# A trunk kernel's inverses by transposes of 128 rows, and its output projection with two operand halves side by side

## The chip, the cores and the metric

The kernel runs on one core of a Trainium2 chip. The metric is the device time of one execution in microseconds. The kernel before has a median of 2547.64 us over 3 runs (2542.07 to 2549.25). One more execution was profiled; all durations below are from it.

## The reference

A two-layer backbone over 256 latent tokens and 256 context tokens, width 2048, in float32. The even layer joins neighbourhood attention (8 heads) and multi-head latent attention (8 heads), gated by SiLU. The odd layer is a bidirectional chunked gated DeltaNet with 32 value heads and chunks of 64 tokens; only the latent tokens leave it. At the end stands an RMSNorm. For the change two pieces matter:

```python
lmat = jnp.where(strict, jnp.einsum('bhncd,bhnsd->bhncs', kb, kf) * decay, 0.0)
rhs = jnp.concatenate([vf * bf[..., None], kb * jnp.exp(gf)[..., None]], axis=-1)
sol = lax.linalg.triangular_solve(lmat + jnp.eye(CHUNK, dtype=F32), rhs, left_side=True, lower=True)
...
o = rmsnorm(o.transpose(0, 2, 1, 3), o_norm)
return (o.reshape(b, t_len, DN_MIX_WIDTH) * jax.nn.silu(z)) @ w_out
```

The first solves a unit lower triangular system of 64x64 for each head, chunk and direction; the kernel computes the inverse matrices instead. The second is the output projection from 4096 to 2048 channels over the 256 latent tokens.

## The kernel before

Activations lie with channels on the 128 partitions and tokens along the columns. A float32 product is made of three matmuls in a reduced format: both operands are split into a high part and a remainder, and `dense` adds high x high (L90), high weight x remainder (L91) and remainder weight x high (L92) into one PSUM tile. Weights come by DMA in pieces of 128x1024 (`raw`, four buffers); ScalarE (ACT) makes the high part (`whi`, L77 or L1091), VectorE (DVE) the remainder (`wlo`, L78 or L1099). The high and remainder parts of the activations are two tiles of 128 x 16 x 512 numbers, `hh` and `hl`; `ch` and `qr`, and `gh` and `gl`, later take the same two places (tags "hh" and "hl"). A place is free for its next tile when the last reader of the tile before is done.

The run has these stages, with their time in the profiled execution:

- Up to about 700 us: layer-one projections and the neighbourhood attention. At its end `ch` (the latent projections in two parts, L451 and L452) and `qr` (rope queries; its unused rows are filled with zeros by L464) take the places of `hh` and `hl`.
- 700 to 880 us: latent attention, eight heads. The last heads read `qr` in the scores (L348). Then `gh` (L485) and `gl` (L486) are made from the gated results `goA` and `goB`.
- 880 to 1110 us: the first output projection, by 512 columns, and the norm of layer two.
- 1110 to 1760 us: the DeltaNet heads. For each of 16 key heads: projections of k and q with convolution (L566) and activation, then the strictly triangular products of a chunk, `NT` (L744), and the intra-chunk products `sp` (L746). Two heads together give 32 matrices of 64x64 for one `inverse`, eight inverses in all. A scheduler in the framework sets the order on each engine, from the code's order and its own model of durations; within one engine the order is fixed in the built program, and an instruction that waits holds everything behind it on that engine.
- 1760 to 2420 us: the scan over chunks, with its order written out by hand for PE, DVE and ACT; its last steps (58 to 69) also hold the first part of the output projection, `early`: eight units by 24 k-steps.
- 2420 to 2549 us: the rest of the output projection (eight units by 8 k-steps, eight by 32, alternating), the final norm and the stores.

An `inverse` works on all 128 partitions: a diagonal block of 32x32 of the two in a 64x64 matrix stands on the upper 64 partitions in columns 0 to 31 (block 0), on the lower 64 in columns 32 to 63 (block 1). Two transposes of 64 rows (L764) bring the blocks into `L`, so that 31 elimination steps (L778 and L780) run along the free dimension on all matrices at once. POOL multiplies the result `X` by the betas (L782; in the last inverse DVE does). Four more transposes of 64 rows, two by L785 and two by L787, put X and its transpose into `U`, each block back in its own columns. PE makes the off-diagonal block from products (L798 and L815), ACT copies it into `U` (L819), and `by_chunk` (L591) stores `U` to `spu` in DRAM, in eight DMAs of 32 rows by 4 KB. The scan loads `spu` in pieces of 64 columns (256 bytes): `ra`, `rb`, `re`.

In the output projection the operand is `hh` and `hl` seen as 32 k-blocks of 256 tokens; `dense` there issues three matmuls of 256 columns per k-step. `project` (L617) adds a unit's PSUM tile, times the gate, to the residual, in two DVE operations of 128x128.

```python
for b in range(2):
    r = slice(64 * b, 64 * b + 64)
    V.transpose(L[r], NTu[r, :, 32 * b:32 * b + 32].rearrange("p u i -> p i u"))
...
def by_chunk(dst, src):
    for b in range(2):
        for h in range(2):
            nc.sync.dma_start(dst[64 * h + 32 * b:64 * h + 32 * b + 32], src[quad(b, h)])
```

Of the kernel before, what the change touches and what calls it, by code (L numbers as in the profile page):

```python
# [26 lines left out]
def trunk_kernel(ctx: ExitStack, tc: tile.TileContext, g):  # L27
# [57 lines left out]
    def dense(ps, w, off, kt, xh, xl, k0=0, sl=slice(0, T), first=True, last=True):  # L85
        for k in range(kt):
            c = off + k * 128
            wh, wl = w[c // 1024]
            c = slice(c % 1024, c % 1024 + 128)
            PE.matmul(ps, wh[:, c], xh[:, k0 + k, sl], start=first and k == 0, stop=False)  # L90
            PE.matmul(ps, wh[:, c], xl[:, k0 + k, sl], start=False, stop=False)  # L91
            end = PE.matmul(ps, wl[:, c], xh[:, k0 + k, sl], start=False, stop=last and k == kt - 1)  # L92
        return end.ins

    def sliced(wsrc, units, k0, n, xh, xl, pst, first, last):
# [134 lines left out]

    hh = big.tile([128, KT, T], F32R, name="hh", tag="hh")
    hl = big.tile([128, KT, T], F32R, name="hl", tag="hl")
    x1d = scratch("x1d", [128, KT, S])
# [68 lines left out]
    with tc.tile_pool(name="ab", bufs=2, reuse_waits="tile") as tp, \  # L302
# [141 lines left out]
        na7 = na_head(7)  # L444
        ch = big.tile([128, KT, T], F32R, name="ch", tag="hh")
        qr = big.tile([128, KT, T], F32R, name="qr", tag="hl")
        for i, gain in enumerate((q_gain, kv_gain)):
# [31 lines left out]
        pace = 0  # L479
        gh = big.tile([128, KT, T], F32R, name="gh", tag="hh")  # L480
        gl = big.tile([128, KT, T], F32R, name="gl", tag="hl")
        for k in range(KT):
# [22 lines left out]
        rb = rstd_bcast(blocks_of(qacc, sq), 4, D, ps, "st", tp)  # L505
        hh = big.tile([128, KT, T], F32R, name="hh", tag="hh")
        hl = big.tile([128, KT, T], F32R, name="hl", tag="hl")
        modulate(1, lambda k, s: x1[s][:, k], rb, hh, hl, tp)
# [104 lines left out]
    def project(u, p):  # L613

        for t in range(2):
            x = x_of[u].rearrange("p (c i) -> p c i", c=4)[:, pair(t)]
            V.scalar_tensor_tensor(x, p[:, t * 128:t * 128 + 128].rearrange("p (h i) -> p h i", h=2),  # L617
                                   mods[1][:, 32 + u, 0:1], x, op0=ALU.mult, op1=ALU.add)


    with tc.tile_pool(name="dn", bufs=2, reuse_waits="tile") as tp, \
# [130 lines left out]
        def inverse(sg):  # L752
# [6 lines left out]
            L = tp.tile([128, 32, 32], F32, name="L", tag="L", bufs=1)  # L759
            P.memset(U[64:128, 0, 0:16, 0:32], 0.0)  # L760
            P.memset(U[0:64, 1, 16:32, 32:64], 0.0)
            for b in range(2):
                r = slice(64 * b, 64 * b + 64)
                V.transpose(L[r], NTu[r, :, 32 * b:32 * b + 32].rearrange("p u i -> p i u"))  # L764
                yield
            bt = tp.tile([128, 2, 8, 2], F32, name="bt", tag="bt", bufs=1)
            V.tensor_tensor(bt, bst[:, sg].rearrange("p a k s h -> p a (k s) h"),
# [14 lines left out]
            (V if sg == 7 else P).tensor_tensor(X, X, bv.unsqueeze(2).broadcast_to([128, 32, 32]), op=ALU.mult)  # L782
            for b in range(2):
                r, c = slice(64 * b, 64 * b + 64), slice(32 * b, 32 * b + 32)
                V.transpose(U[r, 0, :, c].rearrange("p u i -> p i u"), X[r])  # L785
                yield
                V.transpose(U[r, 1, :, c].rearrange("p u j -> p j u"), X[r].rearrange("p i j -> p j i"))  # L787
                yield

# [19 lines left out]
            for u in range(16):  # L809
                for d in range(2):  # L810
                    for h in range(2):
                        r2 = quad(1, h)
                        out = quad(0, h) if d == 0 else r2
                        ab = Xs[d][r2, u], U[r2, 0, 16 * d + u, hi]
                        PE.matmul(pu[d][out, u], ab[d], ab[1 - d], start=True, stop=True,  # L815
                                  tile_position=(r2.start, out.start))
            for d in range(2):
                out, off = (slice(0, 64), hi) if d == 0 else (slice(64, 128), lo)
                A.copy(U[out, d, 16 * d:16 * d + 16, off], pu[d][out])  # L819
            yield  # L820
            for d in range(2):
                by_chunk(spu[sg][:, d], U[:, d, 16 * d:16 * d + 16])

# [308 lines left out]

        gh, gl = [t.rearrange("p k (a s) -> p (k a) s", a=2) for t in (hh, hl)]

# [16 lines left out]
        def early():  # L1151
            done = None
            for i, (u, c) in enumerate(wo_order):
                if c == 0:
                    p = mm_tile()[:, :S]
                for k, _ in enumerate(tile_mm(p, NV + i, 8 * c, gh, gl, XS, c == 0, c == 2)):
# [231 lines left out]
```

## Time and profile before

| | |
|---|---|
| median of 3 runs | 2547.64 us (2542.07 to 2549.25) |
| profiled execution | 2550.65 us, span 2548.9 us |
| mean granted TensorE clock | 0.985 |
| PE, DVE, ACT, POOL busy | 2448.6, 1853.5, 1140.4, 275.6 us |
| DMA | 394.30 MB, mean 155 GB/s |
| 1245 to 1616 us, five inverses | 371 us |

The span is the time from the first to the last instruction; the execution's own time is 1.75 us longer. A group's row names the source line, the engine, the operation, out<-in, the shapes, the count, then busy time and mean ns of one, then the engine's idle time before it and what ended that. A timeline's row begins with start and duration in us; in brackets stands the idle time before it and what ended it. Line numbers are those of the kernel before, unless a text says otherwise.

### The profile page before, as it was taken

How to read it: one execution, taken by the hardware profiler on the slowest of the kernel's cores; microseconds unless marked ns; L12 is line 12 of the kernel's file. 1: busy time of each engine (PE TensorE's matmuls, PEld its weight loads, DVE VectorE, ACT ScalarE, POOL GpSimd, SP SyncE). 2: the span in 40 equal slices, each digit the busy share in tenths (PEclk: the TensorE clock that was granted, in tenths of full speed). 3: DMA queues.
4: the chain of work that ended last, by engine and by line, in shares of the span. 5: the costliest groups of instructions: out<-in, count | busy, mean ns of one | idle time of the engine just before them, and what ended most of it. 6: DMA issues, size and time to landing. Idle time of an engine off the chain costs nothing.

```text
span 2548.9 us, 43398 instructions
## 1 busy us (share of the span) xinstructions
PE 2448.6 (96%) x16586; PEld 2002.5 (79%) x16586; DVE 1853.5 (73%) x3547; ACT 1140.4 (45%) x2468; POOL 275.6 (11%) x261
## 2 busy tenths in 40 slices
PE   6999999999999999999999989899999999999998
PEld 4557888888768778768888888797777777778898
DVE  4644788873456688758999999997777777777654
ACT  4223323233344422377656665543444444445443
POOL 0000000000000000033322332300000000003000
PEclk9999999999999999999999999999999999999999
DMA  8872645532253367645454544573233333335454
GB/s 251 285 267 83 199 163 172 180 127 91 71 198 112 112 216 225 222 155 160 140 167 148 172 145 156 163 211 104 87 107 110 113 103 105 112 93 180 152 188 141
DMA packets 201809, 394.30 MB, mean 155 GB/s; under 512 B 68224, under 2 KB 109696, under 8 KB 201472
## 3 DMA queue, kind: packets, MB, share of 16 engines
q1 hardware_dynamic: 200448, 389.98, 48.7%
q8 instruction: 131, 2.15, 0.3%
q10 hardware_dynamic: 1152, 1.54, 0.2%
q14 instruction: 78, 0.64, 0.1%
HBM read 356.28 MB, written 35.13 MB: 154 GB/s over the span
## 4 chain that ended last, share of the span: by engine, by line
PE 74%; DVE 12%; issue 6%; DMA 4%; ACT 3%; POOL 0%; SPq 0%; DVEq 0%; POOLq 0%; ACTq 0%
PE mm L90 19%; PE mm L91 17%; PE mm L92 17%; PE pks L993 3%; PE pmod L127 3%; DVE wlo L78 3%; PE ptr L1005 2%; DVE acc L566 2%; PE sp L348 2%; DVE outer L778 1%; PE po L348 1%; DVE X L780 1%; DMA mraw<-dn_wm 1%; DVE U L787 1%; PE ptr L1038 1%
## 5 line engine op out<-in xcount | busy, mean ns | idle before, releaser
L90 PE MATMUL mm<-hh,whi 128*128 128x512 f32 (+1 forms) x2784 | 987.0, 355 | 2.4 <-ACT t L643 2.3
L92 PE MATMUL mm<-hh,wlo 128*128 128x512 f32 (+1 forms) x2784 | 959.3, 345 | 12.2 <-DVE wlo L78 11.5
L91 PE MATMUL mm<-hl,whi 128*128 128x512 f32 (+1 forms) x2784 | 959.7, 345 | 0.0
L77 ACT CAST whi<-raw 128x1024 fp32r<-128x1024 f32 (+2 forms) x346 | 337.6, 980 | 650.5 <-PE mm L91 521.4
L90 PEld LDWEIGHTS mm<-hh,whi 128*128 128x128 f32 x2784 | 534.1, 192 | 112.6 <-issue 33.3
L92 PEld LDWEIGHTS mm<-hh,wlo 128*128 128x128 f32 x2784 | 533.2, 192 | 77.1 <-DVE wlo L78 13.1
L91 PEld LDWEIGHTS mm<-hl,whi 128*128 128x128 f32 x2784 | 534.4, 192 | 62.5 <-issue 9.7
L78 DVE TENSOR_TENSOR wlo<-raw,whi 128x1024 fp32r<-128x1024 f32 (+2 forms) x346 | 400.6, 1160 | 204.0 <-ACT whi L77 201.4
L163 DVE SCALAR_TENSOR_TENSOR lacc<-mraw,cond,lacc 128x512 f32<-128x512 f32 x300 | 208.3, 744 | 0.0
L566 DVE SCALAR_TENSOR_TENSOR acc<-cin,taps,acc 128x508 f32<-128x508 f32 (+3 forms) x256 | 191.9, 750 | 7.6 <-ACT acc L557 5.2
L1015 DVE SCALAR_TENSOR_TENSOR vl<-ptr,egm,vh 128x128 fp32r<-128x128 f32 x224 | 64.6, 346 | 98.2 <-ACT rf L1012 39.3
L720 POOL TENSOR_TENSOR rhs<-ghl,incl 128x512 fp32r<-128x512 f32 (+1 forms) x96 | 113.1, 1193 | 186.6 <-PE pd L722 165.9
L778 DVE SCALAR_TENSOR_TENSOR outer<-L,bv,X 128x31 f32<-128x31 f32 (+15 forms) x248 | 118.1, 476 | 5.1
L127 PE MATMUL pmod<-mraw,cond 128*32 128x512 f32 (+2 forms) x640 | 95.6, 504 | 26.4 <-DMA mraw<-ab_wm 19.1
L1099 DVE TENSOR_TENSOR wlo<-raw,whi 128x1024 fp32r<-128x1024 f32 x84 | 102.5, 1220 | 14.0 <-ACT whi L1091 13.4
L194 POOL TENSOR_TENSOR rs<-ms,half 128x4 f32<-128x4 f32 (+1 forms) x5 | 4.7, 949 | 978.6 <-DVE ms L192 978.6
L580 ACT ACTIVATE ac<-acc 128x128 f32<-128x128 f32 x160 | 37.4, 300 | 153.2 <-DVE acc L566 153.1
L780 DVE TENSOR_TENSOR X<-X,outer 128x31 f32<-128x31 f32 (+15 forms) x248 | 101.1, 408 | 4.9
L90 PE MATMUL mm<-gh,whi 128*128 128x512 f32 x256 | 100.4, 394 | 1.7 <-DVE x1B L498 1.7
L91 PE MATMUL mm<-gl,whi 128*128 128x512 f32 x256 | 100.6, 393 | 0.2 <-DVE gl L486 0.2
L92 PE MATMUL mm<-gh,wlo 128*128 128x512 f32 x256 | 100.1, 392 | 0.0
L1009 ACT ACTIVATE vh<-ptr,egm 128x128 fp32r<-128x128 f32 x224 | 71.2, 374 | 60.7 <-PE ptr L1005 58.9
(290 smaller groups left out, 3562.7 us busy)
## 6 DMA issues: line engine op xcount, KB each, us to landing
raw<-dn_w SPq DMA_DIRECT2D x194, 512.0 KB, 4.1
mraw<-dn_wm SPq DMA_DIRECT2D x96, 512.0 KB, 4.7
mraw<-ab_wm SPq DMA_DIRECT2D x88, 512.0 KB, 5.7
raw<-ab_w SPq DMA_DIRECT2D x66, 512.0 KB, 3.8
raw<-dn_wo SPq DMA_DIRECT2D x64, 512.0 KB, 3.7
raw<-ab_wo SPq DMA_DIRECT2D x32, 512.0 KB, 4.8
raw<-ab_w SPq DMA_DIRECT2D x32, 256.0 KB, 3.5
spt<-sp SPq DMA_DIRECT2D x64, 128.0 KB, 2.2
```

The lines of the kernel that those rows point to most:

```text
L77: A.copy(hi[:, :m], raw[:, :m])
L78: V.tensor_tensor(lo[:, :m], raw[:, :m], hi[:, :m].bitcast(F32), op=ALU.subtract)
L90: PE.matmul(ps, wh[:, c], xh[:, k0 + k, sl], start=first and k == 0, stop=False)
L91: PE.matmul(ps, wh[:, c], xl[:, k0 + k, sl], start=False, stop=False)
L92: end = PE.matmul(ps, wl[:, c], xh[:, k0 + k, sl], start=False, stop=last and k == kt - 1)
L127: PE.matmul(pmod[32 * q:32 * q + 32, :m], cond[:, 4 * kg + q, :], raw[c // 1024][:, half + c % 1024:half + c % 1024 + m], start=kg == 0, s ...
L163: V.scalar_tensor_tensor(acc[:, s], raw[:, q], cond[:, k, s:s + 1], acc[:, s], op0=ALU.mult, op1=ALU.add)
L566: V.scalar_tensor_tensor(o3[:, :, i0:i1], p3[:, :, i0 + d:i1 + d], taps[:, ch, t:t + 1], o3[:, :, i0:i1], op0=ALU.mult, op1=ALU.add)
L720: P.tensor_tensor(rhs, ghl[i].bitcast(F32)[:, d, kh * 8:kh * 8 + 2 * n].unsqueeze(2).broadcast_to(sh), incl[:, c].unsqueeze(1).broadcast_t ...
L778: V.scalar_tensor_tensor(o, L[:, rows, k:k + 1].broadcast_to([128, n, m]), bv[:, k:k + 1], X[:, k:k + 1, cols].broadcast_to([128, n, m]), ...
L780: V.tensor_tensor(X[:, rows, cols], X[:, rows, cols], o, op=ALU.subtract)
L1099: V.tensor_tensor(w, raws[j], h.bitcast(F32), op=ALU.subtract)
```

## The change

It has two parts.

**Inverses.** A DMA on SP's queue first copies columns 32 to 63 of `NT` on the lower 64 partitions to columns 0 to 31 there, in 64 x 32 pieces of 128 bytes. The diagonal blocks of all rows then stand in the same columns, and one transpose of 128 rows fills `L`. After the elimination one transpose of 128 rows each puts X and its transpose into columns 0 to 31 of `U`; the off-diagonal blocks go to columns 32 to 63. The lower half's columns are put in order by the store: four DMAs of 32 rows by 4 KB and eight of 32 x 16 pieces of 128 bytes replace the eight DMAs. The transpose into `L` comes after three steps of the generator instead of none; an inverse keeps its number of steps.

**Output projection.** `hh` and `hl`, `ch` and `qr`, `gh` and `gl` each become two halves of one tile with the tag "hx". `dense2` multiplies the high weight with both halves in one matmul of 512 columns, and the weight's remainder with the high half into the first 256 columns. `project` then adds four pieces of 128x128 instead of two. The last unit after the scan stays with `dense`.

```diff
+    def dense2(ps, w, off, kt, x, k0=0, first=True, last=True):
+        p2 = ps.rearrange("p (c s) -> p c s", c=2)
+        for k in range(kt):
+            c = off + k * 128
+            wh, wl = w[c // 1024]
+            c = slice(c % 1024, c % 1024 + 128)
+            start, stop = first and k == 0, last and k == kt - 1
+            if stop:
+                PE.matmul(p2[:, 0], wl[:, c], x[:, 0, k0 + k], start=False, stop=False)
+            PE.matmul(p2, wh[:, c], x[:, :, k0 + k], start=start, stop=stop)
+            if not stop:
+                PE.matmul(p2[:, 0], wl[:, c], x[:, 0, k0 + k], start=False, stop=False)
...
-    hh = big.tile([128, KT, T], F32R, name="hh", tag="hh")
-    hl = big.tile([128, KT, T], F32R, name="hl", tag="hl")
+    def parts_tile(name):
+        return big.tile([128, 2, KT, T], F32R, name=name, tag="hx")
+
+    hx = parts_tile("hx")
+    hh, hl = hx[:, 0], hx[:, 1]
...
-        ch = big.tile([128, KT, T], F32R, name="ch", tag="hh")
-        qr = big.tile([128, KT, T], F32R, name="qr", tag="hl")
+        cx = parts_tile("cx")
+        ch, qr = cx[:, 0], cx[:, 1]
...
-        gh = big.tile([128, KT, T], F32R, name="gh", tag="hh")
-        gl = big.tile([128, KT, T], F32R, name="gl", tag="hl")
+        gx = parts_tile("gx")
+        gh, gl = gx[:, 0], gx[:, 1]
...
     def project(u, p):
-        for t in range(2):
-            x = x_of[u].rearrange("p (c i) -> p c i", c=4)[:, pair(t)]
-            V.scalar_tensor_tensor(x, p[:, t * 128:t * 128 + 128].rearrange("p (h i) -> p h i", h=2),
+        for i in range(p.shape[-1] // 128):
+            x = x_of[u].rearrange("p (c i) -> p c i", c=4)[:, pair(i % 2)]
+            V.scalar_tensor_tensor(x, p[:, i * 128:i * 128 + 128].rearrange("p (h i) -> p h i", h=2),
...
-            P.memset(U[64:128, 0, 0:16, 0:32], 0.0)
+            nc.sync.dma_start(NTu[64:128, :, 0:32], NTu[64:128, :, 32:64])
+            P.memset(U[64:128, 0, 0:16, 32:64], 0.0)
             P.memset(U[0:64, 1, 16:32, 32:64], 0.0)
-            for b in range(2):
-                r = slice(64 * b, 64 * b + 64)
-                V.transpose(L[r], NTu[r, :, 32 * b:32 * b + 32].rearrange("p u i -> p i u"))
+            for _ in range(3):
                 yield
+            V.transpose(L, NTu[:, :, 0:32].rearrange("p u i -> p i u"))
+            yield
...
-            for b in range(2):
-                r, c = slice(64 * b, 64 * b + 64), slice(32 * b, 32 * b + 32)
-                V.transpose(U[r, 0, :, c].rearrange("p u i -> p i u"), X[r])
-                yield
-                V.transpose(U[r, 1, :, c].rearrange("p u j -> p j u"), X[r].rearrange("p i j -> p j i"))
-                yield
+            V.transpose(U[:, 1, :, 0:32].rearrange("p u j -> p j u"), X.rearrange("p i j -> p j i"))
+            yield
+            V.transpose(U[:, 0, :, 0:32].rearrange("p u i -> p i u"), X)
+            yield
...
-                        ab = Xs[d][r2, u], U[r2, 0, 16 * d + u, hi]
+                        ab = Xs[d][r2, u], U[r2, 0, 16 * d + u, lo]
...
-                out, off = (slice(0, 64), hi) if d == 0 else (slice(64, 128), lo)
-                A.copy(U[out, d, 16 * d:16 * d + 16, off], pu[d][out])
+                out = slice(64 * d, 64 * d + 64)
+                A.copy(U[out, d, 16 * d:16 * d + 16, hi], pu[d][out])
             yield
             for d in range(2):
-                by_chunk(spu[sg][:, d], U[:, d, 16 * d:16 * d + 16])
+                src = U[:, d, 16 * d:16 * d + 16]
+                for h in range(2):
+                    nc.sync.dma_start(spu[sg][64 * h:64 * h + 32, d], src[quad(0, h)])
+                    for i, o in ((lo, hi), (hi, lo)):
+                        nc.sync.dma_start(spu[sg][64 * h + 32:64 * h + 64, d, :, o], src[quad(1, h)][:, :, i])
...
+                if sl is XS:
+                    dense2(p, [tuple(wt[j])], 128 * k, 1, gx, k0=k0 + k, first=first and k == 0, last=last and k == 7)
+                    yield
+                    continue
...
-            p = (mm_tile() if i % 2 else ps.tile([128, T], F32, name="mm2", tag="ks"))[:, :S]
-            dense(p, w, 0, 32 - k0, gh, gl, k0=k0, sl=XS)
+            p = mm_tile() if i % 2 else ps.tile([128, T], F32, name="mm2", tag="ks")
+            if i < KT - 1:
+                dense2(p, w, 0, 32 - k0, gx, k0=k0)
+            else:
+                p = p[:, :S]
+                dense(p, w, 0, 32 - k0, gh, gl, k0=k0, sl=XS)
```

The scheduler places the moved instructions anew. In the rows below, of the built programs, the changed kernel's lines are its own: its L583 is L566 of before, L761 is L744, L763 is L746, L783 is L764, L790 is L771, L797 and L799 are L778 and L780, L802 and L804 stand for L787 and L785; L392 is L375, L357 is L340, L409 is L392, L468 is L451, L481 is L464 and L502 is L485.

First DVE, where inverse 3 ends and inverse 4 begins. Before, the last elimination step, then all six transposes in a row:

```order
L778 SCALAR_TENSOR_TENSOR outer<-L,bv,X 128x31
L780 TENSOR_TENSOR X<-X,outer 128x31
L764 STREAM_TRANSPOSE L<-NT 64x1024 x2
L785 STREAM_TRANSPOSE U<-X 64x32x32
L787 STREAM_TRANSPOSE U<-X 64x32x32
L785 STREAM_TRANSPOSE U<-X 64x32x32
L787 STREAM_TRANSPOSE U<-X 64x32x32
L771 STREAM_TRANSPOSE bv<-bt 128x32
```

In the changed kernel U's two transposes and the one into L stand apart, with NT's last writes and seven more operations ahead of the latter:

```order
L804 STREAM_TRANSPOSE U<-X 128x32x32
L790 STREAM_TRANSPOSE bv<-bt 128x32
L78 TENSOR_TENSOR wlo<-raw,whi 128x1024
L757 TENSOR_TENSOR QKm<-kk,incl 128x128 x2
L761 TENSOR_TENSOR NT<-DT,kk 128x512 x2
L583 SCALAR_TENSOR_TENSOR acc<-cin,taps,acc 128x255
L729 RECIPROCAL km<-nrm 128x4
L763 TENSOR_TENSOR sp<-DT,QKm 128x256
L763 TENSOR_TENSOR sp<-DTo,QKm 128x256
L583 SCALAR_TENSOR_TENSOR acc<-cin,taps,acc 128x255
L583 SCALAR_TENSOR_TENSOR acc<-cin,taps,acc 128x254 x2
L783 STREAM_TRANSPOSE L<-NT 128x1024
```

The copy of NT has to land between the rows L761 and L783.

Second ACT, near 688 us, where `ch` and `qr` take their places. Before, four zero fills of qr stand ahead of the copy vT:

```order
L340 CAST kT<-mm 128x512
L77 CAST whi<-raw 128x1024
L464 ACTIVATE qr<-ones 64x1024 x4
L392 COPY vT<-mm 128x512
L451 CAST ch<-craw 128x512 x8
```

In the changed kernel six of the eight fills stand behind vT and ch:

```order
L357 CAST kT<-mm 128x512
L77 CAST whi<-raw 128x1024 x2
L409 COPY vT<-mm 128x512
L468 CAST cx<-craw 128x512 x8
L481 ACTIVATE cx<-ones 64x1024 x6
```

The fills have moved past vT and ch.

Third ACT, near 861 to 877 us, at the copies into `gh`. Before, they begin right behind the last head's vT, ahead of its softmax:

```order
L77 CAST whi<-raw 128x1024
L392 COPY vT<-mm 128x512
L485 CAST gh<-goA 128x256
L485 CAST gh<-goB 128x256
L485 CAST gh<-goA 128x256
```

In the changed kernel (gx is the common tile) the softmax comes first:

```order
L409 COPY vT<-mm 128x512
L392 ACTIVATE pr,sm<-sp,mx 128x512
L357 CAST PT<-pt 128x2x128 x2
L392 ACTIVATE pr,sm<-sp,mx 128x512
L357 CAST vt<-pv 128x512
L357 CAST PT<-pt 128x4x128
L392 ACTIVATE pr,sm<-sp,mx 128x256
L502 CAST gx<-goA 128x256
L502 CAST gx<-goB 128x256
```

The copies have moved behind the last head's third exp; its fourth follows after 16 of them.

More of the change, by code (lines that the diff above doesn't have):

```diff
@@ L505, in trunk_kernel @@
         rb = rstd_bcast(blocks_of(qacc, sq), 4, D, ps, "st", tp)
-        hh = big.tile([128, KT, T], F32R, name="hh", tag="hh")
-        hl = big.tile([128, KT, T], F32R, name="hl", tag="hl")
+        hx = parts_tile("hx")
+        hh, hl = hx[:, 0], hx[:, 1]
         modulate(1, lambda k, s: x1[s][:, k], rb, hh, hl, tp)
@@ L1131, in trunk_kernel @@
         x = None
-        gh, gl = [t.rearrange("p k (a s) -> p (k a) s", a=2) for t in (hh, hl)]
+        gx = hx.rearrange("p c k (a s) -> p c (k a) s", a=2)
+        gh, gl = gx[:, 0], gx[:, 1]
         def gate(k, n, go=None):
@@ L1154, in early @@
                 if c == 0:
-                    p = mm_tile()[:, :S]
+                    p = mm_tile()
                 for k, _ in enumerate(tile_mm(p, NV + i, 8 * c, gh, gl, XS, c == 0, c == 2)):
```

## The prediction

> **What bounds the kernel now.** I read the page first: engine shares and the 40 slices. These are its rows for TensorE (PE) and VectorE (DVE), each digit a tenth of a slice of 63.7 us.
>
> ```profile
> PE 2448.6 (96%) x16586; PEld 2002.5 (79%) x16586; DVE 1853.5 (73%) x3547; ACT 1140.4 (45%) x2468; POOL 275.6 (11%) x261
> PE   6999999999999999999999989899999999999998
> DVE  4644788873456688758999999997777777777654
> ```
>
> Over the whole run PE is the bound. In slices 20 to 27, the stage of the heads and inverses, DVE stands at 9 as well, and that is where the change takes DVE work away. So I read that stage by windows, cut at the transposes that end each inverse (length; busy time and count of PE, weight loads, DVE, ACT, POOL; clock; DMA).
>
> ```profile
> 1245.00:1320.00 75.00, 68.90 (x716) 63.41 (x717) 71.81 (x118) 43.66 (x86) 20.07 (x21) 0.93 0.52 159
> 1320.00:1391.00 71.00, 65.35 (x690) 59.30 (x689) 69.04 (x117) 43.56 (x84) 21.31 (x21) 0.95 0.48 149
> 1391.00:1466.00 75.00, 69.11 (x735) 63.25 (x735) 72.67 (x119) 45.84 (x88) 20.34 (x21) 0.98 0.51 159
> 1466.00:1543.00 77.00, 70.11 (x731) 63.78 (x730) 71.57 (x119) 45.57 (x88) 21.64 (x21) 0.96 0.51 155
> 1543.00:1616.00 73.00, 66.35 (x705) 59.62 (x704) 70.42 (x118) 44.57 (x87) 20.83 (x21) 0.98 0.48 149
> 1616.00:1700.00 84.00, 77.12 (x968) 73.54 (x967) 77.49 (x116) 47.46 (x81) 16.64 (x18) 0.94 0.63 192
> 1700.00:1760.00 60.00, 54.04 (x599) 44.27 (x598) 51.49 (x94) 20.94 (x47) 7.51 (x10) 0.91 0.49 130
> ```
>
> The first five of these periods last 74.2 us on average; DVE is busy 71.1 of that and PE 68.0. DVE is idle 3.1 us a period, PE 6.2. The chain that ended last, for 1250 to 1650 us, says the same.
>
> ```profile
> by line: DVE wlo L78 14.3%; issue 9.5%; DVE acc L566 8.6%; DVE outer L778 8.2%; DVE X L780 7.3%; DVE U L787 5.4%; DVE L L764 5.0%; PE mm L90 4.6%; PE mm L92 4.4%; PE mm L91 4.2%; DMA raw<-dn_w 3.3%; ACT whi L77 2.5%; DMA spu<-U 2.4%; DVE NT
> ```
>
> The DVE lines named with a share sum to 48.8%, PE's to 13.2%; two of the transpose lines alone hold 10.4%.
>
> **The transposes.** Their groups, over the whole run, beside the only transpose of 128 rows and a one-column DVE operation:
>
> ```profile
> L787 DVE STREAM_TRANSPOSE U<-X 64x1024 f32<-64x1024 f32 x16 | 34.5, 2158 | 0.0
> L764 DVE STREAM_TRANSPOSE L<-NT 64x1024 f32<-64x1024 f32 x16 | 32.6, 2040 | 0.1
> L785 DVE STREAM_TRANSPOSE U<-X 64x1024 f32<-64x1024 f32 x16 | 31.4, 1961 | 0.3
> L771 DVE STREAM_TRANSPOSE bv<-bt 128x32 f32<-128x32 f32 x8 | 1.7, 212 | 0.3
> L377 DVE RECIPROCAL rc<-sm 128x1 f32<-128x1 f32 x64 | 10.0, 156 | 7.8 <-ACT pr L375 7.8
> ```
>
> Each inverse has two of each: 2 x (2.16 + 2.04 + 1.96) = 12.3 us. Afterwards one of each, over 128 rows, the columns still 1024. No row shows that shape. Bounds: the same duration as 64 rows, 6.16 us saved per inverse, or twice it, nothing saved. The 128-row transpose of 32 columns takes 56 ns more than an operation of one column, 1.8 ns a column, against 2.0 at 64 rows (2040/1024): rows cost nothing, columns do. I take the same duration: 8 x 6.16 = 49.3 us off DVE.
>
> The Trainium skill, "VectorE: DVE Perf Modes", section "The three transpose paths", lists 311 ns for a 128x128 tile in bf16, done as a grid of 32x32 blocks. By it, as an estimate, 1024 columns take 8 x 311 ns = 2.5 us, and the saving would be 39 us instead of 49; the trace's 64-row rows are quicker per column, and no run here shows the 128-row one.
>
> **The copy that makes it possible.** The lower 64 rows of NT are first moved to the columns of the upper ones by a DMA on SP's queue, issued when DVE has written NT; the transpose waits for its landing, and behind the transpose on DVE stand the next weight remainders (wlo), which PE waits for. Pieces and sizes from landings of today, the store's issue time, and the durations of what DVE has in between:
>
> ```profile
> rb<-spu SPq DMA_DIRECT2D x16, 128.0 KB, 3.0
> kt<-spt SPq DMA_DIRECT2D x16, 128.0 KB, 2.2
> rg<-spk SPq DMA_DIRECT2D x16, 256.0 KB, 2.6
> DMA to landing us min/median/max: 1.9/2.5/7.7
> L591 SPq DMA_DIRECT2D spu<-U x64: 302/393/1494, 1246.8 to 1756.5; - x64
> L78 DVE TENSOR_TENSOR wlo<-raw,whi 128x1024 fp32r<-128x1024 f32 x77 | 97.9, 1272 | 8.5 <-ACT whi L77 7.8 <-PE mm L91 0.7
> L566 DVE SCALAR_TENSOR_TENSOR acc<-cin,taps,acc 128x255 f32<-128x255 f32 x20 | 10.0, 501 | 0.0
> L746 DVE TENSOR_TENSOR sp<-DT,QKm 128x256 f32<-128x256 f32 x10 | 6.7, 666 | 0.0
> L746 DVE TENSOR_TENSOR sp<-DTo,QKm 128x256 f32<-128x256 f32 x10 | 4.2, 415 | 0.4 <-ACT DTo L725 0.4
> L782 POOL TENSOR_TENSOR X<-X,bv 128x1024 f32<-128x1024 f32 x7 | 13.4, 1919 | 74.1 <-DVE X L780 74.1
> ```
>
> The load rb comes in 512 pieces of 256 bytes, kt in 128 of 1 KB: 0.8 us for 384 pieces, 2.1 ns each. The copy has 64 x 32 = 2048 pieces of 128 bytes and 256 KB: 2.2 + 1920 x 2.1 ns + 0.4 (rg against kt) = 6.6 us. Bounds: 2.6, what rg takes for the same bytes, and 7.7, the longest landing of any store or load of spu. In the order of the built program, by these durations and the transposes', five of the eight inverses have over 7.5 us of DVE work between NT and the transpose. Inverses 0 and 4 have four L566 and two L746: 4 x 0.50 + 1.08 = 3.1 us; inverse 6 has a wlo more, 4.4. Waits: 2 x 3.5 + 2.2 = 9.2 us. Also, U's transposes wait for POOL's 1.92 us product, which two L transposes (4.1 us) cover today. In inverses 4 and 6 only one wlo (1.27) stands there: about 1.2 us in all. DVE's net: 49.3 - 9.2 - 1.2 = 38.9 us.
>
> SP's queue: the stores of U become 12 instead of 8, eight of them in 128-byte pieces, and with the copy an inverse issues five more, at 0.39 us each 2 us of 75; the weight loads behind them have four buffers and DMA is busy half the time. U is not needed again for a period, and spu not before the scan. I cost them at nothing; uncovered it is 2 x 8 = 16 us, in the range's upper part. The moved memsets keep their size.
>
> **What of it comes through.** A middle period loses 6.16 and gains 10.4/8 = 1.3 of waiting: 4.9 net. With DVE's idle time kept, it would last 69.3 against PE's 68.0 busy, leaving PE 1.3 of its 6.2 us of idle time. PE's busy time is counted too high where lone matmuls stand, so this is not excluded, but waits on ACT, DMA and issue (17.7% of the chain) stay. Bounds: nothing, and all 38.9. I take 65%, between the DVE lines' half of the chain and all: 25.3 us.
>
> **The output projection.** Two matmuls of 256 columns by the same weight half become one of 512. Starts of matmuls in dense runs, nine steps apart in each pair:
>
> ```profile
> 979.85 0.39 PE L90 MATMUL mm<-gh,whi 128*128 128x512 f32 x1
> ...
> 981.89 0.39 PE L90 MATMUL mm<-gh,whi 128*128 128x512 f32 x1
> 2500.07 0.28 PE L90 MATMUL mm<-hh,whi 128*128 128x256 f32 x1
> ...
> 2501.15 0.28 PE L90 MATMUL mm<-hh,whi 128*128 128x256 f32 x1
> ```
>
> A step of 512 takes 2.04/9 = 0.2267 us, one of 256 1.08/9 = 0.120. A k-step falls from 0.360 to 0.3467: 13.3 ns. There are 288 such k-steps after the scan (8 x 8 + 7 x 32, the last unit kept) and 192 in the scan's last steps: 3.8 + 2.6 = 6.4 us. The columns streamed stay the same, hence so little. Where it lies:
>
> ```profile
> 2350.00:2400.00 50.00, 49.87 (x414) 44.67 (x410) 34.53 (x86) 22.79 (x59) 5.96 (x5) 1.00 0.42 133
> 2500.00:2520.00 20.00, 20.00 (x169) 20.00 (x169) 10.47 (x13) 8.83 (x12) 0.00 (x0) 1.00 0.61 184
> L617 DVE SCALAR_TENSOR_TENSOR xo<-mm,mod,xo 128x128 f32<-128x128 f32 x32 | 9.7, 345 | 2.9 <-PE mm L92 2.9
> ```
>
> PE is full in both. DVE adds two L617 a unit, 0.7 us, and is idle 9.5 of 20 and 15.5 of 50 us: hidden; if not, 15 x 0.7 = 10 us. I take 3.8 and, inside the scan, 2.0: 5.8 us.
>
> **Both halves in one buffer.** Their release is now one. Two places:
>
> ```profile
> 688.32 4.26 ACT L464 ACTIVATE qr<-ones 64x1024 fp32r<-64x1024 f32 x4 [4.38 <-PE mm L91]
> 693.10 0.65 PE L354 MATMUL pv<-ident,vT 128*128 128x128 f32 x4 [3.23 <-ACT vT L392]
> 876.71 0.51 PE L348 MATMUL sp<-kr,qr 128*128 128x256 f32 x3
> 879.31 0.50 PE L91 MATMUL mm<-gl,whi 128*128 128x512 f32 x1
> ```
>
> At 688 the zero fills move behind vT and ch: PE's 3.2 us wait goes, but two more fills, 2.1 us, and ch now stand ahead of the softmax that PE needs next. I take 0, between -3 and +1. At 877 the copies into gh, done early today, must wait for the last scores, as gl does already; then 16 of them stand ahead of the last exp, which PE needs after seven matmuls. I take +1.5, between -3 and +4.
>
> **Sum.** 25.3 + 5.8 - 1.5 = 29.6 us. The profiled span 2548.9 becomes 2519.3; that run took 2550.65, 3.0 above the median 2547.64 of the three runs. Forecast: 2547.6 - 29.6 = 2518 us.
>
> **Rivals.**
> - PE takes over: its 68.0 busy us a period, not DVE, decide, and only a third comes through, 13.0 us: 2530. For it: PE is at 92% there too. Against: PE's share of the chain is 13%.
> - All comes through: 38.9 + 6.4 - 1.5 = 43.8, 2504 us.
> - The transposes don't do what they should: 128 rows cost double. DVE saves nothing, waits cost 0.65 x 10.4 = 6.8: 2547.6 + 6.8 - 5.8 + 1.5 = 2550. Against it stands L771's row.
> - Slower: the copy lands late. At 15 us the eight waits are 8 x 15 - (3.1 + 3.1 + 4.4 + 5 x 8) = 69.4, all on DVE with wlo behind: 69.4 + 1.2 - 49.3 - 5.8 + 1.5 = +17, 2565 us. It decides from a landing of 12.9 us, where this sum is zero. For it: no transfer today has 2048 pieces, and SP issues in order. Against it: 7.7 is the longest landing in that row, and DMA is half idle. The Trainium skill, "DMA: Bandwidth & Descriptors", Specifications, speaks for it: below 512 bytes a transfer becomes a read-modify-write; the 256-byte rows here show only 0.8 us.
>
> **How the numbers follow.** Forecast 0.60, PE takes over 0.20, all comes through 0.08, double cost 0.06, late copy 0.06. A measurement tells 0.3%, 7.6 us, from no change. The first three are faster, 0.88, less 0.01 of the second under extra waits: 0.87 faster, 0.07 the same, 0.06 slower. Range: from 2500, the case in which all comes through with some waits missing, to 2541, the PE case with 11 us of the SP or projection costs uncovered; the last two rivals, 0.12, and a few of the lowest are left out.
>
> **What would show it.** Right: transposes of 128x1024 at about 2.0 to 2.2 us, three an inverse; periods of about 71 us; DVE under 67 busy us; copy landing about 6.6 us, with waits in front of inverses 0, 4 and 6; a k-step of 0.347 us. Wrong: transposes of 4 us, a landing over 12 us, or periods still at 74 with PE's idle time unchanged.

## The result and the profile after

| | before | after |
|---|---|---|
| median of 4 runs each, us | 2548.39 (2542.07 to 2549.25) | 2530.81 (2527.79 to 2532.39) |
| ratio, with its 95% interval | | 0.9935 (0.9916 to 0.9954) |
| profiled execution, us (span) | 2550.65 (2548.9) | 2532.22 (2530.4) |

The change takes 17.6 us off; 29.6 were forecast. The page of the changed kernel, engines and two rows of slices (its line numbers are its own from here on):

```profile
PE 2439.8 (96%) x16106; PEld 1968.8 (78%) x16106; DVE 1819.5 (72%) x3569; ACT 1142.9 (45%) x2468; POOL 273.4 (11%) x261
PE   6999999999989999999999899999999999999998
DVE  4644778873455688767999998976677777777765
```

DVE has 34 us less, and only six of its slices still stand at 9. The transposes, by group:

```profile
L802 DVE STREAM_TRANSPOSE U<-X 128x1024 f32<-128x1024 f32 x8 | 18.5, 2315 | 0.1
L783 DVE STREAM_TRANSPOSE L<-NT 128x1024 f32<-128x1024 f32 x8 | 16.3, 2033 | 5.7 <-DMA NT<-NT 5.7
L804 DVE STREAM_TRANSPOSE U<-X 128x1024 f32<-128x1024 f32 x8 | 15.7, 1959 | 0.0
```

They last about as long with 128 rows as with 64 (2315, 2033 and 1959 ns against 2158, 2040 and 1961): 50.5 us for 24 where 48 took 98.5. Ahead of L783 DVE waits 5.7 us for the copy, at two places; ahead of U's transposes it waits for next to nothing (0.1 us). The copy's landings:

```profile
L778 SPq DMA_DIRECT2D NT<-NT x8: 596/601/675, 1171.8 to 1650.7; - x8
DMA to landing us min/median/max: 4.3/5.0/6.4
```

So the edits do what they should. Where did the time go? First the whole stage of the heads and inverses, from the load of its constants (`cumh`) to the first matmul of the scan, of before (length; busy time of PE, weight loads, DVE, ACT, POOL; clock; DMA):

```profile
1113.40:1753.20 639.80, 589.32 (x5999) 534.12 (x5999) 591.94 (x975) 387.13 (x758) 171.11 (x169) 0.96 0.51 156
```

And of the changed kernel, the same stretch, its periods cut at the transposes that end each inverse, its last part, and the scan's first 7 us:

```profile
1114.60:1739.10 624.50, 584.57 (x6000) 529.06 (x5999) 547.40 (x951) 389.26 (x760) 170.20 (x170) 0.97 0.60 166
...
1243.00:1311.00 68.00, 63.22 (x705) 57.85 (x704) 65.53 (x115) 45.81 (x89) 19.17 (x21) 0.97 0.62 174
1311.00:1374.00 63.00, 60.30 (x669) 54.44 (x668) 60.19 (x106) 38.68 (x73) 20.89 (x20) 0.97 0.54 154
1374.00:1444.00 70.00, 64.49 (x702) 58.39 (x700) 64.02 (x109) 43.18 (x78) 19.48 (x20) 0.98 0.59 164
1444.00:1519.00 75.00, 69.62 (x730) 63.74 (x731) 68.77 (x123) 45.84 (x92) 21.00 (x21) 0.95 0.60 163
1519.00:1581.00 62.00, 57.34 (x608) 51.87 (x607) 55.50 (x103) 35.75 (x70) 14.44 (x16) 0.94 0.62 169
...
1670.30:1739.10 68.80, 64.13 (x596) 56.47 (x595) 46.70 (x80) 26.11 (x52) 4.86 (x6) 0.95 0.61 159
1717.00:1739.10 22.10, 22.10 (x342) 18.02 (x340) 10.29 (x12) 10.61 (x25) 3.82 (x4) 1.00 0.60 145
1739.00:1746.00 7.00, 7.00 (x39) 5.30 (x39) 3.28 (x6) 3.05 (x10) 0.00 (x0) 1.00 0.38 113
```

Read each stage as PE's busy time plus PE's idle time. Before: 589.3 + 50.5 = 639.8. After: 584.6 + 39.9 = 624.5. DVE lost 44.5 busy us; 29.2 of them became idle time of DVE (47.9 to 77.1), and 15.3 came off the stage, 10.6 of these as gaps that PE no longer has.

The five middle periods are 67.6 us each against 74.2, shorter than the 71 forecast. But they also hold less of TensorE's work, 315.0 busy us together where it was 339.8. What follows gives that back. Here are ACT's copies that end the last two inverses, before:

```profile
1705.88 1.19 ACT L819 COPY U<-pu 64x512 f32<-64x512 f32 x2 [5.85 <-PE pu L815]
1753.25 1.19 ACT L819 COPY U<-pu 64x512 f32<-64x512 f32 x2 [0.65 <-PE pu L815]
```

and after:

```profile
1669.74 1.19 ACT L836 COPY U<-pu 64x512 f32<-64x512 f32 x2 [3.93 <-PE pu L832]
1730.55 1.19 ACT L836 COPY U<-pu 64x512 f32<-64x512 f32 x2 [0.19 <-PE pu L832]
```

Inverse 6 ends 36.1 us earlier, inverse 7 22.7, and the scan starts 14.1 earlier (1753.20 and 1739.10). Before, the scan started as the last inverse ended; now that inverse ends 8.6 us earlier, and PE still has projections to do. DVE's chain ran ahead; PE's projections did not, and they pile up at the end. From the copy of inverse 6 to the scan PE now has 64.1 busy us, before it had this:

```profile
1706.50:1753.20 46.70, 42.81 (x429) 35.95 (x427) 42.10 (x79) 16.66 (x36) 3.69 (x5) 0.95 0.44 116
1753.00:1760.00 7.00, 7.00 (x38) 4.63 (x29) 3.30 (x6) 3.65 (x9) 0.95 (x1) 0.56 0.78 186
```

That is 21.3 us of work put off, against 22.0 us given back; in the last 22.1 us PE has no gap at all. The second row shows a small gain besides: before, the scan began at a granted clock of 0.56, now at 1.00. The scan's first matmul into `psu` comes 47.0 us after its start instead of 49.6.

Last the output projection: two matmuls of both halves by the weight's high part, nine k-steps apart, from the timeline.

```profile
2479.91 0.40 PE L105 MATMUL mm<-hx,whi 128*128 128x512 f32 x1
...
2483.09 0.40 PE L105 MATMUL mm<-hx,whi 128*128 128x512 f32 x1
```

A k-step takes 3.18/9 = 0.353 us, not 0.347: the 512 columns 0.236, the 256 behind them 0.117 (medians of the starts from there to the end). From the start of the scan's last group of `psu` products to the end the kernel takes 137.9 us, before 139.2. Added up, the two spans differ by 18.5 us: the stage of the heads starts 1.2 us later and is 15.3 shorter, the scan's beginning gives 2.6, its rest 0.5 and the end 1.3.

### The profile page after: what moved, and what is told of

The parts are those of the page before. It is cut to its first block, busy times and chain, and to the rows that moved or that the text cites. A ratio compares the mean times of both kernels' runs of the same rounds, so it can differ in the third digit from the quotient of the medians.

```text
span 2530.4 us, 42502 instructions
## 1 busy us (share of the span) xinstructions
PE 2439.8 (96%) x16106; PEld 1968.8 (78%) x16106; DVE 1819.5 (72%) x3569; ACT 1142.9 (45%) x2468; POOL 273.4 (11%) x261
## 4 chain that ended last, share of the span: by engine, by line
PE 75%; DVE 10%; issue 6%; DMA 4%; ACT 3%; SPq 1%; POOL 1%; DVEq 0%; POOLq 0%; ACTq 0%
PE mm L90 18%; PE mm L91 17%; PE mm L92 16%; PE pks L1014 3%; PE pmod L141 3%; DVE wlo L78 3%; PE ptr L1026 2%; PE sp L365 2%; DVE outer L797 2%; PE mm L105 2%; DVE X L799 2%; DVE acc L583 2%; PE po L365 1%; PE ptr L1059 1%; PE psu L1045 1%
## 5 line engine op out<-in xcount | busy, mean ns | idle before, releaser
L90 PE MATMUL mm<-hx,whi 128*128 128x512 f32 (+1 forms) x2304 | 846.5, 368 | 2.8 <-ACT t L660 2.4
L92 PE MATMUL mm<-hx,wlo 128*128 128x512 f32 (+1 forms) x2304 | 823.0, 357 | 9.5 <-DVE wlo L78 9.5
L91 PE MATMUL mm<-hx,whi 128*128 128x512 f32 (+1 forms) x2304 | 822.8, 357 | 4.7 <-issue 4.7
L78 DVE TENSOR_TENSOR wlo<-raw,whi 128x1024 fp32r<-128x1024 f32 (+2 forms) x346 | 400.8, 1160 | 207.5 <-ACT whi L77 206.2
L90 PEld LDWEIGHTS mm<-hx,whi 128*128 128x128 f32 x2304 | 440.7, 191 | 106.7 <-issue 27.0
L92 PEld LDWEIGHTS mm<-hx,wlo 128*128 128x128 f32 x2304 | 440.4, 191 | 73.5 <-DVE wlo L78 10.9
L91 PEld LDWEIGHTS mm<-hx,whi 128*128 128x128 f32 x2304 | 441.1, 191 | 67.3 <-issue 13.3
L583 DVE SCALAR_TENSOR_TENSOR acc<-cin,taps,acc 128x508 f32<-128x508 f32 (+3 forms) x256 | 199.6, 780 | 18.3 <-ACT acc L574 15.7
L105 PE MATMUL mm<-hx,whi 128*128 128x512 f32 x480 | 173.1, 405 | 0.0
L107 PE MATMUL mm<-hx,wlo 128*128 128x256 f32 x457 | 128.5, 281 | 0.8 <-DVE wlo L1120 0.8
L797 DVE SCALAR_TENSOR_TENSOR outer<-L,bv,X 128x31 f32<-128x31 f32 (+15 forms) x248 | 114.3, 461 | 6.2 <-POOL X L792 0.7
L105 PEld LDWEIGHTS mm<-hx,whi 128*128 128x128 f32 x480 | 89.0, 188 | 24.1 <-issue 4.6
L799 DVE TENSOR_TENSOR X<-X,outer 128x31 f32<-128x31 f32 (+15 forms) x248 | 101.0, 407 | 5.4
L90 PE MATMUL mm<-gx,whi 128*128 128x512 f32 x256 | 99.7, 391 | 2.6 <-DVE x1B L515 1.7
```

The source lines that it names most:

```text
L78: V.tensor_tensor(lo[:, :m], raw[:, :m], hi[:, :m].bitcast(F32), op=ALU.subtract)
L105: PE.matmul(p2, wh[:, c], x[:, :, k0 + k], start=start, stop=stop)
L107: PE.matmul(p2[:, 0], wl[:, c], x[:, 0, k0 + k], start=False, stop=False)
L583: V.scalar_tensor_tensor(o3[:, :, i0:i1], p3[:, :, i0 + d:i1 + d], taps[:, ch, t:t + 1], o3[:, :, i0:i1], op0=ALU.mult, op1=ALU.add)
L797: V.scalar_tensor_tensor(o, L[:, rows, k:k + 1].broadcast_to([128, n, m]), bv[:, k:k + 1], X[:, k:k + 1, cols].broadcast_to([128, n, m]), ...
L799: V.tensor_tensor(X[:, rows, cols], X[:, rows, cols], o, op=ALU.subtract)
```

## The experiments

Theory A says that TensorE's work, not VectorE's, sets the stage of the heads, so that VectorE's saving comes through in part. At first I put it so that TensorE takes over only after the change; the runs moved that. Its rivals are named in the expectations. All times are medians, set against the kernel before as timed beside them (2549.3 to 2550.6 us). The changed kernel itself was timed on another occasion (2530.8 us, ratio 0.9935); so a distance to it is given by the medians and, where it matters, also by the difference of the two ratios.

| run | us | ratio to before (95%) |
|---|---|---|
| inv_alone | 2530.4 | 0.9922 (0.9906 to 0.9937) |
| proj_alone | 2550.0 | 0.9998 (0.9987 to 1.0009) |
| before_lessPE | 2572.8 | 1.0094 (1.0079 to 1.0109) |
| after_lessPE | 2529.9 | 0.9922 (0.9908 to 0.9937) |
| after_z14 | 2527.6 | 0.9909 (0.9883 to 0.9935) |
| before_z14 | 2552.3 | 1.0011 (1.0002 to 1.0021) |
| before_lessDVE | 2538.8 | 0.9953 (0.9938 to 0.9969) |
| after_lessDVE | 2523.6 | 0.9893 (0.9873 to 0.9913) |
| before_morePE | 2579.7 | 1.0115 (1.0092 to 1.0139) |
| after_morePE | 2561.7 | 1.0045 (1.0028 to 1.0062) |
| after_store4k | 2529.1 | 0.9909 (0.9890 to 0.9928) |
| z14_split | 2527.7 | 0.9906 (0.9890 to 0.9923) |

**The two parts apart.** Of the changed kernel, one part each taken back:

```diff
# inv_alone: the inverses as changed, and
-    hx = parts_tile("hx")
...
+    hh = big.tile([128, KT, T], F32R, name="hh", tag="hh")
+    hl = big.tile([128, KT, T], F32R, name="hl", tag="hl")
...
-            if i < KT - 1:
-                dense2(p, w, 0, 32 - k0, gx, k0=k0)
...
+            dense(p, w, 0, 32 - k0, gh, gl, k0=k0, sl=XS)
...
# proj_alone: dense2 and the common tiles, inverse() as before
```

> The change's inverses alone: separate tiles, the output projection as before. Theory A (the heads' stage gives less than forecast because TensorE takes over, about 15 us, and the projection gives the rest): 2547.6 - 15 = 2532 us, the first matmul of the scan about 14 to 16 us earlier than before. Rival B (the inverses bring the forecast 25 us and the common tile or the projection gives some 8 of it back): 2522 us. Rival C (the inverses bring little by themselves, the projection does it): above 2540 us.

> The output projection and the common tiles alone, the inverses as before. Theory A: scan and projection 3 to 4 us shorter, the common tile +1 us: 2544 to 2546 us. Rival B (the common tile costs about 8 us net): 2553 to 2556 us. Rival C (the projection brings most of the gain): 2535 us or less.

The inverses alone take 19.0 us off, as much as the whole change within the intervals; the projection with the common tiles takes nothing that can be measured (0.9998). B and C fall. A expected 15 and, for the projection, 3 to 4 less 1 for the tile; the second is too much, and the section on the prediction shows why.

**Less work for TensorE.** In the projections of the heads' stage one matmul of three is left out.

```diff
-        dense(p[:, :n], w, 0, KT, hh, hl, sl=sl)
+        dense(p[:, :n], w, 0, KT, hh, None, sl=sl)
...
+            if xl is not None:
-            PE.matmul(ps, wh[:, c], xl[:, k0 + k, sl], start=False, stop=False)
+                PE.matmul(ps, wh[:, c], xl[:, k0 + k, sl], start=False, stop=False)
```

> Before, with one of the three matmuls of a k-step left out (high weight by remainder of the activation) in all projections of the heads' stage: about 160 us of TensorE's 589 busy us between 1113 and 1753 us go, VectorE keeps its 592 us in 640. Theory A (VectorE sets the time before, TensorE is near behind): the stage loses 15 to 35 us, its floor being VectorE's 592 us: about 2513 to 2533 us. Rival D (TensorE sets the time before already): the stage loses much more of the time than VectorE's idle 48 us can cover, which its floor forbids; so at that floor, 2500 us.

> The changed kernel with the same matmuls left out. Theory A (TensorE holds back what VectorE saved, since VectorE has 547 busy us in a stage of 624): without TensorE the saving comes through, the distance to the kernel before with the same cut is 35 to 45 us instead of 17. Rival E (waits, on the copy of NT, on POOL, on ScalarE and on weights, hold it back, not TensorE): the distance stays 15 to 20 us.

Every expectation for the first missed: with less work the kernel before is 23.5 us slower. The stage of it, then of the changed kernel with the same cut:

```profile
1107.60:1772.67 665.07, 489.55 (x4966) 421.32 (x4964) 594.86 (x977) 360.29 (x737) 159.04 (x172) 0.80 0.49 150
```

```profile
1110.25:1728.92 618.67, 479.60 (x4838) 410.31 (x4836) 545.44 (x949) 362.88 (x739) 157.63 (x171) 0.82 0.57 165
```

PE is idle 175 us and its clock falls to 0.80, so the cut did not make TensorE as quick as meant, and the scheduler's order differs too. How much of the 23.5 us is due to each was not separated. (The 128 matmuls that the second row has fewer are 32x32 products of the last inverse, which there stand behind the scan's first matmul.) The distance is clear, though: 43.0 us between the two kernels, where DVE has 49.4 busy us less. Where TensorE has gaps all through, a time as large as 87% of VectorE's saving comes through. E, with 15 to 20, falls here, though with TensorE's clock not the same as in the kernels themselves, and PE's busy time is 10 us apart between the two.

**Less work for VectorE.** In both kernels:

```diff
-                V.tensor_tensor(X[:, rows, cols], X[:, rows, cols], o, op=ALU.subtract)
+                if k % 2 == 0:
+                    V.tensor_tensor(X[:, rows, cols], X[:, rows, cols], o, op=ALU.subtract)
```

> The kernel before with the same subtractions left out, as a control. Theory A: 50 us less of VectorE do here what the change's 42 us did: 17 to 24 us off, 2525 to 2532 us, and the distance to the changed kernel with the same cut is 0 to 8 us instead of 19. Rival E: the distance stays 15 us or more.

> The changed kernel with every second subtraction of the elimination left out: 8 x 15 operations of 0.42 us, 50 us of VectorE, as much again as the change took off. Theory A (TensorE now holds the stage): little comes through, 0 to 10 us: 2521 to 2531 us. Rival E (VectorE and its waits still set the periods, with the same share as the change's 42 us that gave 19): 20 to 25 us off, 2506 to 2511 us.

The stage of before with this cut, and of the changed kernel:

```profile
1109.66:1740.46 630.80, 592.89 (x6000) 534.28 (x6000) 556.14 (x855) 382.98 (x754) 183.51 (x170) 0.98 0.52 161
```

```profile
1116.71:1731.75 615.04, 587.18 (x6001) 529.48 (x6000) 508.27 (x831) 387.31 (x758) 188.26 (x170) 0.98 0.60 169
```

DVE's busy time fell by 35.8 and 39.1 us, not 50: in the kernel before the subtractions lost 48.7, but the weight remainders (L78), as many as before, grew from 163.8 to 173.0 us, and other groups changed too. Before lost 11.8 us, a third, less than A's 17; the changed kernel lost 7 to 11 (7.2 by the medians, 10.7 by the ratios), a fifth to a quarter, as A had it. The distance stays 15.1, which A had at 0 to 8 and E at 15 or more; E's 20 to 25 for the changed kernel did not come. So A in its first form is wrong: no corner shows between the two kernels at which TensorE takes over. The share that comes through was already small before.

**More work for TensorE** asks whether TensorE sets the time before as well. One 256-column matmul per k-step is issued twice in the query projections.

```diff
-        dense(p[:, :n], w, 0, KT, hh, hl, sl=sl)
+        dense(p[:, :n], w, 0, KT, hh, hl, sl=sl, twice=U_Q <= u < U_Z)
...
+            for _ in range(2 if twice else 1):
-            PE.matmul(ps, wh[:, c], xl[:, k0 + k, sl], start=False, stop=False)
+                PE.matmul(ps, wh[:, c], xl[:, k0 + k, sl], start=False, stop=False)
```

> The kernel before, with the matmul of high weight by remainder issued twice in the 16 query projections of the heads' stage: 16 x 16 x 0.12 us = 31 us more for TensorE, nothing for VectorE. Theory A (TensorE's work sets the stage already before the change, VectorE only makes it wait; so VectorE's cuts come through at a quarter to a third): most of it comes through, 20 to 31 us, 2569 to 2581 us. Rival G (VectorE sets the periods before, TensorE has 50 us of slack in the stage): 0 to 10 us, 2549 to 2560 us.

> The changed kernel with the same 31 us more for TensorE. Theory A: 20 to 31 us, 2551 to 2562 us, much as in the kernel before. Rival G: TensorE has only just become the bound, so here nearly all comes through, 25 to 31 us, against 0 to 10 in the kernel before.

31 us more for TensorE cost 30.4 us in the kernel before and 30.9 in the changed one (29 and 28 by the ratios). The stage of before with it:

```profile
1112.10:1786.10 674.00, 625.07 (x6256) 567.66 (x6255) 599.23 (x975) 391.87 (x760) 176.14 (x170) 0.96 0.48 150
```

PE's busy time grew by 35.8 us and its idle time stayed at 48.9 (50.5): next to none of the new work went into the gaps. In the changed kernel the stage is this:

```profile
1110.83:1764.61 653.78, 622.17 (x6256) 565.89 (x6256) 551.50 (x951) 396.67 (x764) 183.86 (x170) 0.97 0.57 159
```

There the busy time grew by 37.6 us and the stage by 29.3, so some 8 us went into gaps, which fell from 39.9 to 31.6. G falls in the kernel before (0 to 10 us); for the changed kernel both theories allow what was measured. So work added to TensorE comes through whole, or nearly, on either side of the change, and work taken off VectorE by a fifth to a little over two fifths (19.0 of 43.7 for the inverses alone). That is what theory A now says, and so much is shown. Not shown is what work added to VectorE would cost: no run adds any, and work taken off TensorE gave no gain at all. That either engine, given more, would lengthen the stage in full is therefore not excluded.

**The last stretch.** `ZH`, the number of key heads whose gate units are worked during the first seven inverses, from 13 to 14, in both kernels.

```diff
-        ZH = 13
+        ZH = 14
```

> The changed kernel with one pair of gate units (two projections of 256 columns, 11.5 us of TensorE) moved from the last inverse's stretch into the seven before (ZH 14 for 13). Theory A (the last inverse ends 22.7 us earlier but the scan starts only 14.1 us earlier, because TensorE still has projections to do and is full from 1717 to 1739 us): the units fit into the 23 us that TensorE idles in the five middle periods, and 4 to 8 us come back: 2523 to 2527 us. Rival E (waits, not TensorE's work, set the last stretch): no gain, 2530 us or more.

> The same move in the kernel before, as a control. Theory A: before, the inverses end where the scan starts and VectorE sets them; two more units of VectorE work (2 x 2 x 1.27 us) in the earlier periods lengthen those and shorten the last: 2546 to 2552 us, no gain. Rival F (the move is good for either kernel, whatever the inverses do): 4 to 8 us off here too, 2541 to 2545 us.

The changed kernel gets 3.2 us faster by the medians, 6.6 by the ratios; before gets 1.7 to 2.8 slower. The signs are A's, and F falls. In the trace of after_z14 the stage is 4.6 us shorter, and the scan again starts as the last inverse ends (1735.8 us, its copy at 1736.1). But the ratio's interval overlaps the changed kernel's, so that this version beats it is likely and not certain, and E's no gain is not excluded by the times alone.

**The copy and the stores.**

```diff
# z14_split: ZH = 14, and in head(), behind each write of NT
+                n = NTs[sg][64:128, d, k2].rearrange("p s h i -> p (s h) i")
+                nc.sync.dma_start(n[:, :, 0:32], n[:, :, 32:64])
...
-            nc.sync.dma_start(NTu[64:128, :, 0:32], NTu[64:128, :, 32:64])
# after_store4k
-                for h in range(2):
-                    nc.sync.dma_start(spu[sg][64 * h:64 * h + 32, d], src[quad(0, h)])
-                    for i, o in ((lo, hi), (hi, lo)):
-                        nc.sync.dma_start(spu[sg][64 * h + 32:64 * h + 64, d, :, o], src[quad(1, h)][:, :, i])
+                by_chunk(spu[sg][:, d], src)
```

> The changed kernel with the gate units moved as in the run with ZH 14, and NT's copy in four parts, each issued as soon as its quarter of NT is written, three of them before the last; 14.2 us of VectorE's waits for the copy stand in that run. Theory A: the waits fall below 5 us and a third of it comes through, 3 us: 2523 to 2526 us. Rival E (waits on the copy come through whole): 10 us off, 2517 us.

> The changed kernel with U stored as before, eight DMAs of 32 rows by 4 KB (the lower half's columns then stay in the wrong order). It prices the eight stores in 128-byte pieces. Theory A (stores lie beside other work): within 2 us of the changed kernel, 2529 to 2533 us. Rival H (SP's queue, five more issues an inverse, delays the weights): 5 to 10 us off, 2521 to 2526 us.

The store in large pieces gives 2529.1 us against 2530.8, 1.8 us less by the medians and 6.6 by the ratios (0.9909 against 0.9935, with intervals that overlap). That leaves both A's 2 us and the lower end of H: what the small pieces cost lies between nothing and some 6 us. The split copy did not do what it was to do. Its transposes of L, with DVE's wait ahead of them:

```profile
L784 DVE STREAM_TRANSPOSE L<-NT 128x1024 f32<-128x1024 f32 x8 | 16.3, 2036 | 18.2 <-DMA NT<-NT 9.3 <-DMA spt<-sp 8.8
```

and those of after_z14:

```profile
L783 DVE STREAM_TRANSPOSE L<-NT 128x1024 f32<-128x1024 f32 x8 | 16.2, 2031 | 14.2 <-DMA NT<-NT 14.2
```

The wait grew to 18.2 us. So the run can't tell what a shorter wait brings. But 4 us more of it cost nothing that can be measured (2527.65 against 2527.63), and after_z14 itself waits 8.5 us more than the changed kernel without being slower. Both fit A, by which such waits fall into time that DVE has to spare.

## Why the prediction was right and wrong

Faster was right, and the cause of it too: the inverses give VectorE less to do, and part of that shortens the stage. The sum was 12 us too large, because more was expected to come through than did. The measured time is that of the rival "PE takes over", which had a chance of 0.20 against the forecast's 0.60; it lies in the range because the range was drawn to hold that rival. By its steps:

- **The transposes.** Forecast 49.3 us off DVE, measured 98.5 - 50.5 = 48.0. That 128 rows would cost no more than 64, read from one small transpose of 128 rows, holds within some 7%: 2315, 2033 and 1959 ns. The 2.5 us that stood beside it as an estimate were too much.
- **The copy.** Forecast a landing of 6.6 us and waits of 9.2 at inverses 0, 4 and 6; measured 5.0 (4.3 to 6.4) and 5.7, at inverses 0 (1.7) and 4 (3.9) alone. POOL's product, 1.2 us in the sum, is not waited for by U's transposes (0.1 us of idle time). SP's extra issues, costed at nothing, cost between nothing and some 6 us (after_store4k). DVE's net is thus 48.0 - 5.7 = 42.3 instead of 38.9: up to here the sum was, if anything, too low. The rival of a late copy, with landings of 15 us, did not come near (6.4 at most).
- **What of it comes through.** This is the step that failed. I took 65%, between DVE's half of the chain and all. With the inverses alone 19.0 us of 42.3 came, 45% (38 to 57% by the interval), and 2.6 of the 19.0 are the scan's quicker start at a higher clock, which the sum did not have. The rival "PE takes over" gave the time that came, 2530 us, and its reason is the one that stands, with one correction: work added to PE comes through before the change as well. What misled me was the chain that ended last, with DVE lines at half and PE at 13%, and the 9s in both rows of slices. The chain says who released whom, not what a microsecond less would bring: with 31 us more for TensorE the kernel before took 30.4 us longer, although DVE's lines held more of its chain.
- **The bound on idle time.** PE was idle 6.2 us a period, and the whole saving in the stage had to come out of that or out of PE's busy time, which a better clock can shorten, since PE's matmuls in the stage stay (5999 and 6000). 25 us would have needed half of the stage's 50.5 idle us; 10.6 came, and 4.7 of busy time. The prediction had this number, named it as not excluding the forecast, and went on.
- **The output projection.** 13.3 ns a k-step was mis-sized: measured 0.3600 - 0.3533 = 6.7 ns, after the scan 288 x 6.7 ns = 1.9 us instead of 3.8. Inside the scan's last steps 2.0 us were forecast; with and without `dense2` the scan's end lies 653.4 and 653.7 us behind its start, 0.3. The durations were taken from dense runs of one shape (0.2267 and 0.120 us); alternating, the two shapes took 0.236 and 0.117.
- **Both halves in one buffer.** 1.5 us were put down. proj_alone, in which this loss and the projection's gain stand together, is even with before to 0.1%, so the times don't resolve it. The profiles do. From the start of the last score matmul to the end of the last matmul on `gh` and `gl` it is 186.7 to 188.3 us in the six profiled kernels with separate tiles and 189.6 to 193.6 in the eight with the common tile: 4.1 us more on average, the upper end of what was put down for the place at 877 us. Up to those scores the common tile is 0.9 us ahead on average, with overlapping values. So the term is about 3.2 us, and it takes back what the projection brings.

Together: 19.0 for the inverses, in which the stores' cost is contained, 1.9 and 0.3 for the projection, less 3.2 for the common tile, make 18.0 us against 17.6 measured. That they agree so closely is luck, as the interval of the 19.0 alone is some 4 us to either side.

## What to carry to other kernels

When two engines look full in a stage, neither the slices nor the chain tell what a microsecond on either is worth; add a known piece of work to each, take one off, and see how much of it comes back (here VectorE was given no more work, which leaves the picture half open). A saving on the engine that only makes the other one wait can bring little more than that other engine's gaps, and of those only the ones behind that wait. And look at what is left to do when the quicker chain ends: here the inverses ended 36 us earlier, and the projections that had been put off filled 21 of them.

## What the hardware showed besides

**TensorE's clock after gaps.** In before_lessPE stands this row:

```profile
1268.00:1308.00 40.00, 21.29 (x328) 15.90 (x329) 34.77 (x61) 15.54 (x35) 14.56 (x18) 0.51 0.24 63
```

PE has long waits here, 9.97 us up to 1270.11 and 7.76 up to 1297.65, and its granted clock is about half. The clock does not follow the busy share from slice to slice: by windows it is 0.50 from 1270 to 1274 us, where PE is busy 3.9 of 4.0 us (with 32x32 products), and 0.50 from 1290 to 1297.5, where it does nothing. Near the end a projection starts (from the timeline, with the two long waits ahead):

```profile
1270.11 3.46 PE L799 MATMUL px<-U,NT 32*32 32x32 f32 x122 [9.97 <-DVE U L788]
...
1297.65 1.51 PE L737 MATMUL kk<-sp 128*32 128x128 f32 x32 [7.76 <-ACT sp L709]
1300.25 1.12 PE L690 MATMUL ptk<-ident,ac 128*128 128x128 f32 x4 [1.09 <-ACT ac L578]
1303.52 0.58 PE L90 MATMUL mm<-hh,whi 128*128 128x256 f32 x1 [2.15 <-ACT acc L558]
1303.90 0.42 PE L93 MATMUL mm<-hh,wlo 128*128 128x256 f32 x1
...
1306.88 0.41 PE L93 MATMUL mm<-hh,wlo 128*128 128x256 f32 x1
1307.10 0.36 PE L90 MATMUL mm<-hh,whi 128*128 128x256 f32 x1
1307.29 0.28 PE L93 MATMUL mm<-hh,wlo 128*128 128x256 f32 x1
1307.41 0.28 PE L90 MATMUL mm<-hh,whi 128*128 128x256 f32 x1
```

Starts lie 0.21 us apart, from 1307.29 on 0.12: after 3.6 us of dense matmuls the clock is back at full. The Trainium skill, "TensorE: Matmul & The Clock Gate", Part 1, gives about 3.4 us of sustained work for this; the trace agrees, for this projection; the 32x32 products at 1270 us, nearly as long, did not bring the clock back, and why stays open. So the waits here cost more than their length: an estimate from these starts is 17 x 0.09 us = 1.5 us. Some of what the change gained is of this kind: the stage's mean clock went from 0.96 to 0.97, the scan's first 7 us from 0.56 to 1.00.

**A copy's landing hardly depends on its pieces here.** In z14_split a quarter of NT, 512 pieces of 128 bytes, lands in 4.4 us (median of 32); in after_z14 the whole, 2048 pieces, in 5.2 (median of 8). My 2.1 ns a piece, from two loads, would have made the difference 3.2 us.
